# Hybrid decoder block: rotary tables made early, with the sine's table set loaded near the beginning, the rows filled in v's ring and the transposes in the middle of the first accumulation

## The chip, the cores and the metric

The kernel runs on one core of a Trainium2 chip. The metric is the device time of one execution in microseconds (us). A profiled execution also gives a span, which begins with the first and ends with the last instruction of the core.

## The reference, cut to what matters

One layer of a decoder block, for one sequence of 1024 tokens of width 1024. The conditioning vector gives six modulation vectors; the first two scale and shift the normalised input.

```
cond = silu(c);  mod = cond @ w_ada + b_ada          # six parts
h    = rms_norm(x, g_attn_pre) * (1 + sc_a) + sh_a
proj = h @ w_in                                      # q, k, v of mixers A and B
ang  = positions * inv_freq                          # 8 frequencies
q, k = partial_rope(q, k, cos(ang), sin(ang))        # first 16 of 64 dims
oa   = sliding-window attention with sinks           # 8 query, 2 key heads
ob   = mixture of three dilated windows              # 8 heads
x    = x + gt_a * rms_norm(concat(norm(oa), norm(ob)) @ w_out)
x    = x + gt_m * rms_norm(relu(h2 @ w_up)**2 @ w_down)
```

All of it is float32 in and out. The kernel multiplies each operand as a high and a low half, three matmuls to a product.

## The kernel before, in words

**A planner writes the order.** `Sched` (L175) holds a queue for each of ScalarE (ACT), VectorE (DVE), GpSimd (POOL) and the DMA queue (SP), and several streams for TensorE (PE). Each step, made by `op` (L196) or `pe_op` (L208), has a duration that the author wrote down, the events that it depends on, the ring buffers that it takes and gives back (`Res`, L161), and a priority. `run` (L272) advances model clocks and emits whichever step can start first; the priority only breaks ties. So the written durations decide the order in which instructions stand on each engine, and an edit early in the program can reorder what follows. Once emitted, an engine works strictly in that order, and waits at its head for semaphores.

**The opening stage.** SP loads `x` in eight blocks of 128 tokens, the first 2048 columns of `w_ada` in sixteen pieces and the first unit's weights (`order0`, L471). `x_block` (L610) squares a block on ACT (L613), makes 1/rms on POOL (`rsqrt_mean`, L452: L457 and L459), scales the block on ACT or DVE (L617, L618), transposes it on PE (L625) and copies it to `xnT` (L629). `mod_group(g)` (L634), g from 0 to 3, sums `w_ada` times `cond` on DVE (L645, L647), adds over partitions on PE (L655), makes scale and shift on DVE (L661 to L663), and calls `mod_chunk` (L672) for the chunks k = 2g and 2g+1 of the model width: high half on ACT (L684), full value on ACT (L681), low half on DVE (L687). `split_w` (L536) splits the weights, with the high half on ACT (L539) and the low half on DVE or POOL (L544).

**The first unit's accumulation.** `first_unit` (L883) keeps six accumulators in PSUM: x = 0, 1 (token halves) by c = 0, 1, 2 (128 columns each). Chunks k = 0 to 5 are added as they come; the chunks 6 and 7 follow tile by tile, starting with x = 0, c = 0 (the tail). Each chunk and tile is two matmuls with the high half of h (L861, L862) and one with the low half (L864). PE fills idle time before that with matmuls on ones (`filler`, L871, L878). One of the two buffers of the PSUM pool `pt` belongs to an accumulator from the second half of chunk 0 on.

**The rotary tables.** DVE reduces the angles (`f_turns`, L590). `f_sin` (L604) makes sine (L605) and cosine (L606) and then runs an Exp (L607), so that the table set of Exp is back in place. It waits for the angles and for all of `e_xn`, with priority 8. DVE negates the sine (L697). `tables` (L700) then, for the cosine and the sine: POOL sets a tile `rows` (L707) and copies the 8 columns to their places, ten copies each (L713); PE transposes it in two groups of four, one for each x (L719); ACT scales each group into `tab` (L721). The tile comes from the ring "wa" of `p0` (six buffers). A second call (L949), for mixer B, comes with unit 2.

**Behind a tile.** `evac` (L734): for c = 0 DVE rotates the PSUM tile with the tables (L757 to L760, the rope), ACT makes the high half (L763), DVE or POOL the low half (L766). For c = 1, 2 ACT and DVE make the halves (L774, L777). The halves `hl` lie in the ring "stg" of five tiles, which the loads of the second part of `w_ada` (`wa_st`, L994) use as well. SP then copies them row by row into `kt` and `qt` (L803): twelve DMAs for each x of the first unit. The v part goes through ACT (`vt`, L825), PE (L831) and ACT and DVE (L839, L842) into the ring "v" of three buffers. `proj_tile` (L915) makes the tiles of the units 1 to 5 in the two buffers of the pool `pj`, L861 to L864 again.

**Attention** opens (`open_attention`, L955) when the tables and all chunks are planned; it loads the masks (L971). The first scores (L1177) need all twelve DMAs of unit 0, x = 0. After them the matmuls of the projections and those of attention alternate, and the output projection and the MLP follow. The MLP is made of seven half-size products (P1 to P7) in place of eight for each block (L1897 to L1899).

## Time and profile before

| what | us |
|---|---|
| median of three runs (1161.61 to 1167.61) | 1163.08 |
| the profiled execution's own time | 1161.99 |
| its span | 1160.2 |
| PE busy | 1117.1 |
| first unit's projection, last matmul issued | 66.94 |
| unit 1's first two tiles, last matmul issued | 77.10 |
| first scores | 83.00 |

The opening stage is the first 67 us. The matmuls of the other projections (L861 into `pj`) stand from 67.2 to 391.4 us, beside attention; those of the output projection (L1473) from 413 to 530; the MLP's begin at 530. A row of the timeline gives start, length, engine, line, operation, output and inputs, count, and in brackets the idle time of the engine before it and what ended that. A matmul's length overlaps with the next: distances between starts are what they cost.

### The profile page before, as it was taken

To read this page: it belongs to the slowest core of one execution; us is meant where nothing else is said; L and a number is where in the kernel's file an instruction comes from. 1 tells how busy PE (TensorE), PEld (TensorE's weight loads), DVE (VectorE), ACT (ScalarE), POOL (GpSimd) and SP (SyncE) were. 2 spreads that over 40 slices of the span, in tenths; PEclk is the share of its full clock that TensorE was granted. 3 is DMA by queue.
4 is the path that set the end of the run, shared out by engine and by line. 5 is a ranking of instruction groups with operands and counts; after the bars stand their busy time and mean duration, and the time that the engine had idled before them with its cause. 6 is when DMAs were issued, how large, how long until landed. Compare 5 with 4: busy or idle time off the path is not lost.

```text
span 1160.2 us, 15646 instructions
## 1 busy us (share of the span) xinstructions
PE 1117.1 (96%) x5416; PEld 926.6 (80%) x5416; DVE 815.4 (70%) x1380; ACT 639.2 (55%) x1105; POOL 261.1 (23%) x344
## 2 busy tenths in 40 slices
PE   8989989999999899998999999999999999999996
PEld 7768778788888787887788888888888888888885
DVE  7848576566666775658969665499653796547998
ACT  7949676455555774667676524563233732246542
POOL 2347667566663441112000000000000000000002
PEclk9989989999999989999999999999999999999998
DMA  9477857465545614554683057812369212585103
GB/s 351 161 174 168 168 120 182 111 153 122 134 102 130 156 48 139 193 181 182 257 314 118 19 207 274 315 50 89 120 220 326 106 55 73 184 306 181 37 19 146
DMA packets 90944, 185.31 MB, mean 160 GB/s; under 512 B 8432, under 2 KB 31088, under 8 KB 90864
## 3 DMA queue, kind: packets, MB, share of 16 engines
q1 hardware_dynamic: 90864, 184.30, 51.1%
q8 instruction: 43, 0.70, 0.3%
q14 instruction: 37, 0.30, 0.1%
HBM read 137.08 MB, written 28.31 MB: 143 GB/s over the span
## 4 chain that ended last, share of the span: by engine, by line
PE 70%; DVE 10%; DMA 7%; issue 4%; POOL 4%; ACT 3%; SPq 2%; DVEq 0%; POOLq 0%; ACTq 0%
PE mlp_ps L1898 16%; PE mlp_ps L1899 16%; PE mlp_ps L1897 16%; PE pj L861 3%; PE pj L864 3%; PE pj L862 3%; PE s_ps L1122 2%; PE o_ps L1257 1%; DMA wa<-in_w_ada 1%; SPq L803 1%; PE pt_ps L1227 1%; DMA wa_st<-in_w_ada 1%; DVE hw L1668 1%; PE pt_ps L1230 1%; PE s_ps L1177 1%
## 5 line engine op out<-in xcount | busy, mean ns | idle before, releaser
L1897 PE MATMUL mlp_ps<-hw 128*128 128x512 f32 x896 | 349.7, 390 | 1.2 <-ACT hw L1659 1.2
L1898 PE MATMUL mlp_ps<-hw 128*128 128x512 f32 x896 | 348.7, 389 | 1.1 <-DVE hw L1665 1.1
L1899 PE MATMUL mlp_ps<-hw 128*128 128x512 f32 x896 | 348.6, 389 | 0.0
L1897 PEld LDWEIGHTS mlp_ps<-hw 128*128 128x128 f32 x896 | 168.2, 188 | 36.8 <-ACT hw L1659 1.6
L1898 PEld LDWEIGHTS mlp_ps<-hw 128*128 128x128 f32 x896 | 168.2, 188 | 36.8 <-DVE hw L1665 1.4
L1899 PEld LDWEIGHTS mlp_ps<-hw 128*128 128x128 f32 x896 | 168.2, 188 | 34.9
L1668 DVE TENSOR_TENSOR hw<-w,hw 128x1024 fp32r<-128x1024 f32 x96 | 114.5, 1219 | 94.7 <-ACT hw L1661 94.4
L1661 ACT CAST hw<-w 128x1024 fp32r<-128x1024 f32 x96 | 97.5, 1047 | 129.8 <-PE mlp_ps L1899 97.5
L1997 POOL TENSOR_TENSOR st<-st,nhalf 128x1 f32<-128x1 f32 x8 | 7.8, 978 | 601.9 <-DVE st L1995 601.9
L861 PE MATMUL pj<-hw,w_hl 128*128 128x512 f32 x240 | 104.2, 434 | 0.0
L864 PE MATMUL pj<-hw,w_hl 128*128 128x512 f32 x240 | 95.5, 398 | 0.0
L862 PE MATMUL pj<-hw,w_hl 128*128 128x512 f32 x240 | 95.3, 397 | 0.0
L1245 DVE TENSOR_TENSOR ph<-pt_ps,ph 128x512 fp32r<-128x512 f32 (+1 forms) x110 | 69.7, 648 | 36.0 <-ACT ph L1241 35.7
L1661 ACT CAST hw<-u 128x1024 fp32r<-128x1024 f32 x48 | 48.7, 1052 | 64.6 <-PE mlp_ps L1899 64.6
L1241 ACT CAST ph<-pt_ps 128x512 fp32r<-128x512 f32 (+1 forms) x110 | 59.5, 555 | 32.1 <-PE pt_ps L1230 27.0
L1668 DVE TENSOR_TENSOR hw<-u,hw 128x1024 fp32r<-128x1024 f32 x48 | 57.0, 1218 | 18.2 <-ACT hw L1661 18.2
L1148 ACT ACTIVATE p_sb<-p_sb,mn 128x128 f32<-128x128 f32 (+3 forms) x64 | 49.7, 777 | 36.3 <-DVE mn L1141 34.9
L1955 DVE TENSOR_TENSOR yacc<-yacc,mlp_ps 128x512 f32<-128x512 f32 x96 | 62.1, 681 | 3.3 <-PE mlp_ps L1899 3.3
L1153 POOL TENSOR_SCALAR p_sb<-p_sb,den 128x128 f32<-128x128 f32 (+3 forms) x64 | 49.0, 775 | 47.8 <-DVE den L1151 44.6
L1010 POOL TENSOR_TENSOR ada_acc<-ada_acc,wa_st 128x512 f32<-128x512 f32 x42 | 55.5, 1320 | 3.5
L864 PEld LDWEIGHTS pj<-hw,w_hl 128*128 128x128 f32 x240 | 45.6, 190 | 10.7
L1473 PE MATMUL y_ps<-hw,oh 128*128 128x512 f32 x128 | 51.7, 404 | 0.0
(205 smaller groups left out, 2010.6 us busy)
## 6 DMA issues: line engine op xcount, KB each, us to landing
hw<-s_dram SPq DMA_DIRECT2D x84, 512.0 KB
wa_st<-in_w_ada SPq DMA_DIRECT2D x32, 512.0 KB
w<-in_w_up SPq DMA_DIRECT2D x32, 512.0 KB
w<-in_w_down SPq DMA_DIRECT2D x32, 512.0 KB
s_dram<-hw SPq DMA_DIRECT2D x28, 512.0 KB
w_st<-in_w_in SPq DMA_DIRECT2D x36, 256.0 KB
x_sb<-in_x SPq DMA_DIRECT2D x16, 512.0 KB
wa<-in_w_ada SPq DMA_DIRECT2D x32, 256.0 KB
```

What stands on the lines that cost most here:

```text
L861: T.matmul(ps, w[:, 0, n], h[0], start=(k == 0), stop=False)
L862: T.matmul(ps, w[:, 1, n], h[0], start=False, stop=False)
L864: T.matmul(ps, w[:, 0, n], h[1], start=False, stop=(k == KC - 1))
L1010: G.tensor_tensor(ada.acc[:, :512], ada.acc[:, :512], wa[:, j], ALU.add)
L1241: A.copy(b["ph"][:, 0, :w], b["pt"][:, :w])
L1245: V.tensor_tensor(b["ph"][:, 1, :w], b["pt"][:, :w], b["ph"][:, 0, :w].bitcast(F32), ALU.subtract)
L1661: A.copy(out[j][0], flat(src[j]))
L1668: V.tensor_tensor(out[j][1], flat(src[j]), out[j][0].bitcast(F32), ALU.subtract)
L1897: T.matmul(ps[m][:], sh, mh, start=starts and k == 0, stop=False, **kw)
L1898: T.matmul(ps[m][:], sh, ml_, start=False, stop=False, **kw)
L1899: T.matmul(ps[m][:], sl, mh, start=False, stop=k == 3, **kw)
L1955: e = op("DVE", t_dv(512), lambda: V.tensor_tensor(y(), y(), ps[m][:], ALU.add), [e, ml.e_y[tb, n]], gives=gives, prio=1)
```

## The change

The changed kernel adds two steps and moves three.

- A new step loads the table set of the sine: one activation with Sin on a small constant tile, behind the first Exp (the silu) and the initialisation, priority 0.
- `f_sin` no longer waits for `e_xn`. It waits for the angles and the step above, with priority 1, and its trailing Exp is gone. The negation follows it, also with priority 1.
- A new step with priority 8 runs an Exp on the small tile, behind the sine and the low halves of chunk 7. It brings the table set of Exp back.
- The first call of `tables` takes its `rows` from the ring "v" instead of "wa". Filling them waits for the sine and for all eight 1/rms steps of `x_block`. The transposes also wait for the high half of chunk 3 (`e_hh[3, 1]`). Both calls' transposes get that event; for the second call it is long past.

```diff
+    warm = p0.tile([P, KC], F32, name="warm")
+    e_sinset = op("ACT", 1.5, lambda: A.activation(warm[:], nhalf[:], AF.Sin), [e, e_init], prio=0)
...
     def f_sin():
         A.activation(sinw[:, :, 1], ang[:], AF.Sin)
         A.activation(cosw[:], kq[:], AF.Sin)
-        A.activation(ang[:], kq[:], AF.Exp)
-    e_ang, e_xn = e, [[], []]
+    e_xn, e_rs = [[], []], []
+    e_sin = op("ACT", 0.5, f_sin, [e, e_sinset], prio=1)
+    e_rope = op("DVE", 0.15, lambda: V.tensor_scalar(sinw[:, :, 0], sinw[:, :, 1], -1.0, None, ALU.mult), [e_sin],
+                prio=1)
...
         e = rsqrt_mean(rstd[:, tb:tb + 1], ssq[:, tb:tb + 1], e)
+        e_rs.append(e)
...
-    e = op("ACT", 3.2, f_sin, [e_ang] + e_xn[0] + e_xn[1], prio=8)
-    e_rope = op("DVE", 0.15, lambda: V.tensor_scalar(sinw[:, :, 0], sinw[:, :, 1], -1.0, None, ALU.mult), [e],
-                prio=8)
...
-                t = b["t"] = place()[:].rearrange("p (b r) -> p b r", b=TB)
+                t = b["t"] = place(i)
...
-            e = op("POOL", 4.0, f_rows, [e_rope], takes=[(r_place, 1)], prio=0)
+            e = op("POOL", 4.0, f_rows, [e_rope] + e_rs, takes=[(r_place, 1)] if r_place else [], prio=0)
...
-                d = pe_op("tab", 0.43, f_t, [e], takes=[(r_bank, 1)], gives=[(r_place, 1)] if x else [])
+                d = pe_op("tab", 0.43, f_t, [e, e_hh[3, 1]], takes=[(r_bank, 1)], gives=[(r_place, 1)] if x and r_place else [])
...
-    tables([(0, 2, 4), (1, 2, 1)], lambda: place0("rows"), r_wa, r_t,
+    tables([(0, 2, 4), (1, 2, 1)], lambda i: vring.tile([P, TB, P], F32, name="rows", tag="v"), r_v, r_t,
            lambda: pt.tile([P, 4, P], F32, name="ptab", tag="t"), [[], []])
+
+    op("ACT", 1.6, lambda: A.activation(warm[:], nhalf[:], AF.Exp), [e_sin] + [e_hl[KC - 1, x] for x in range(2)],
+       prio=8)
```

More of the change, by code (lines that the diff above doesn't have):

```diff
@@ L948, in feed_proj @@
                     e_.clear()
-                tables([(0, 1, 4)], lambda: stage("rows"), r_stg, r_x,
+                tables([(0, 1, 4)], lambda i: stage("rows")[:].rearrange("p (b r) -> p b r", b=TB), r_stg, r_x,
                        lambda: px.tile([P, 4, P], F32, name="ptab", tag="x"), [[e_rot[1, 0]], [e_rot[1, 1]]])
```

## The prediction

> **What bounds the kernel now.** I read the page's first lines, then the windows of the first 200 us, because the change touches the opening stage and what follows from it.
>
> ```profile
> span 1160.2 us, 15646 instructions
> ...
> PE 1117.1 (96%) x5416; PEld 926.6 (80%) x5416; DVE 815.4 (70%) x1380; ACT 639.2 (55%) x1105; POOL 261.1 (23%) x344
> ```
> ```profile
> 36.00:57.00 21.00, 21.00 (x100) 17.62 (x101) 17.74 (x29) 18.84 (x22) 9.82 (x21) 1.00 0.42 136
> 57.00:67.00 10.00, 10.00 (x54) 8.25 (x52) 6.13 (x10) 5.87 (x11) 3.44 (x3) 1.00 0.44 152
> 67.00:77.30 10.30, 10.30 (x48) 8.07 (x46) 3.56 (x6) 3.33 (x8) 7.31 (x10) 1.00 0.82 183
> 77.30:83.00 5.70, 0.18 (x1) 0.03 (x1) 1.55 (x3) 0.52 (x1) 0.00 (x0) 0.82 0.85 182
> 83.00:90.00 7.00, 7.00 (x30) 5.72 (x31) 4.27 (x17) 4.24 (x15) 2.84 (x6) 0.66 0.80 157
> 90.00:120.00 30.00, 29.49 (x176) 25.13 (x175) 26.19 (x83) 27.39 (x81) 24.58 (x41) 1.00 0.77 177
> 120.00:200.00 80.00, 74.34 (x398) 61.50 (x396) 51.64 (x146) 55.06 (x145) 53.18 (x85) 0.96 0.68 154
> ...
> 143.50:148.70 5.20, 0.18 (x1) 0.00 (x0) 3.79 (x10) 4.58 (x10) 3.42 (x4) 0.72 0.31 100
> 148.70:153.00 4.30, 4.29 (x19) 3.89 (x20) 1.99 (x9) 1.97 (x8) 4.17 (x9) 0.54 0.41 100
> ```
>
> Columns: stretch, length, busy PE, weight load, DVE, ACT, POOL, then PE's granted clock. PE is busy without a break from 36 to 77, stands still for 5.5 us, works 7 us at a mean clock of 0.66, and is full again until 143.5, where a second stop comes. So the time is PE's work plus its stops, and a stop costs twice: 7.00 x (1 - 0.66) = 2.4 us after the first, 4.30 x (1 - 0.54) = 2.0 us after the second. A change in the opening stage is worth what it takes from or adds to PE's waits. Past about 200 us the orders of both kernels agree on every engine but for a few swaps, so the rest (MLP included) only shifts.
>
> The timeline shows what the first stop waits for, in PE, DVE and SP rows.
>
> ```profile
> 57.09 0.60 PE L719 MATMUL ptab<-head,rows 128*128 128x128 f32 x4
> 57.44 0.48 PE L861 MATMUL acc<-hw,w_hl 128*128 128x512 f32 x1
> ...
> 59.04 0.48 PE L864 MATMUL acc<-hw,w_hl 128*128 128x512 f32 x1
> ...
> 83.00 1.94 PE L1177 MATMUL s_ps<-kt,qt 128*128 128x128 f32 x8 [5.51 <-DMA kt<-hl]
> ...
> 148.71 0.69 PE L831 MATMUL pv<-head,vt 64*128 64x64 f32 x4 [5.02 <-ACT tab L721]
> ```
> ```profile
> 62.57 0.68 DVE L757 TENSOR_TENSOR hl<-acc,tab 64x512 f32<-64x512 f32 x1 [3.70 <-ACT tab L721]
> ```
> ```profile
> 64.81 0.44 SPq L994 DMA_DIRECT2D wa_st<-in_w_ada  x1
> ...
> 67.47 1.78 SPq L803 DMA_DIRECT2D kt<-hl  x2
> 69.31 8.35 SPq L803 DMA_DIRECT2D qt<-hl  x10
> 77.75 1.32 SPq L803 DMA_DIRECT2D kt<-hl  x2
> 79.16 7.46 SPq L803 DMA_DIRECT2D qt<-hl  x10
> ```
> The chain of waits has the last of the twelve by itself:
>
> ```profile
> 77.06 0.59 SPq L803
> ```
>
> The tile of x = 0, c = 0 is complete at about 59.4 (the L864 at 59.04 ends it), but its rope starts at 62.57, when the sine's table arrives from ACT. SP then issues the twelve DMAs of x = 0 from 67.47 to 77.66, and the scores start at 83.00. The tables are late by 3.1 us, and the scores hang on them.
>
> **The change, part by part.**
>
> *The sine on ACT.* Rows of ACT, POOL and DVE:
>
> ```profile
> 5.60 1.06 ACT L613 ACTIVATE junk<-x_sb 128x1024 bf16<-128x1024 f32 x1 [1.05 <-DMA x_sb<-in_x]
> ...
> 32.60 1.55 ACT L684 ACTIVATE hw<-xnT,s_a,g_a 128x512 fp32r<-128x512 f32 x2
> ...
> 37.71 2.37 ACT L681 ACTIVATE xnT<-xnT,s_a,g_a 128x1024 f32<-128x1024 f32 x2
> ...
> 41.13 1.28 ACT L605 ACT_TABLE_LOAD   x1
> 42.42 0.26 ACT L605 ACTIVATE sinw<-ang 128x64 f32<-128x64 f32 x1
> ...
> 42.84 1.28 ACT L607 ACT_TABLE_LOAD   x1
> 44.14 0.26 ACT L607 ACTIVATE ang<-kq 128x64 f32<-128x64 f32 x1
> 44.88 2.38 ACT L684 ACTIVATE hw<-xnT,s_a,g_a 128x1024 fp32r<-128x1024 f32 x2 [0.48 <-DVE s_a L663]
> ```
> ```profile
> 28.10 0.57 POOL L459 TENSOR_TENSOR rstd<-rs_t,nhalf 128x1 f32<-128x1 f32 x1
> ...
> 42.96 4.77 POOL L713 COPY rows<-cosw 128x64 f32<-128x64 f32 x10 [9.00 <-ACT cosw L606]
> 47.67 0.95 POOL L707 MEMSET rows<- 128x1024 f32 x1
> 48.69 3.02 POOL L713 COPY rows<-sinw 128x64 f32<-128x64 f32 x4
> 52.49 1.14 POOL L713 COPY rows<-sinw 128x64 f32<-128x64 f32 x6 [0.78 <-DVE sinw L697]
> ...
> 63.12 1.29 POOL L544 TENSOR_TENSOR w_hl<-w_st,w_hl 128x512 fp32r<-128x512 f32 x1 [0.16 <-ACT w_hl L539]
> ```
> ```profile
> 46.89 1.52 DVE L647 SCALAR_TENSOR_TENSOR acc_a<-wa,cond,acc_a 128x512 f32<-128x512 f32 x2
> ```
>
> Two table loads and the small activations behind them leave ACT at 41.13 to 44.40. ACT then stood idle for 0.48 us until DVE's shift came, so their going is worth nothing by itself. Early, one load and a tiny activation fall before 5.60, where ACT idled 1.05 us: the first square moves by about 0.35 us. The two sines (0.5 us) come behind the angles. I walked ACT, DVE, POOL and PE through the new order with these durations: ACT's lead on the first chunks is up to 1.4 us later, the planner gives DVE one scaling more, and by the second half of chunk 0 ACT is even again (32.2 against 32.6) while DVE is 0.8 us late, which puts PE about 0.7 us behind. The last `w_ada` loads slip by 0.7 us too; DVE uses the last of them at 46.89, well after they land, so that is covered. The third load (1.28 us) now stands on ACT ahead of two splits and the rope's cast, behind the last chunk, where ACT waits anyway: nothing.
>
> The Trainium skill, "ScalarE: Activation LUTs", section "What ACT_TABLE_LOAD costs", counts a drain of about 1.38 us on top of each load. The row at 42.42 starts 0.01 us behind the load, and no drain is seen; with it the first square would be 1.4 us later still, and the sum worse by at most that.
>
> *The rows on POOL* now start behind the eighth 1/rms, at about 28.9. A copy took 0.48 us (4.77 / 10) beside a busy DVE, 0.755 (3.02 / 4) beside DVE's low halves, 0.19 (1.14 / 6) with DVE idle. With 0.48 the cosine is ready at 28.9 + 0.95 + 4.8 = 34.7 and the sine, at something between 0.48 and 0.755, at 40.5 to 43.2. PE asks for them at 38.0 and 42.2: a wait of 0 to 1.0, taken as 0. At 0.755 throughout, the sine is ready at 28.9 + 1.9 + 15.1 = 45.9.
>
> *The transposes on PE.* Four groups of 0.35 us (57.44 - 57.09) leave the tail and go to chunks 1 and 2: 1.4 us earlier work, none saved. In the middle they share one PSUM buffer, so each waits for ACT's copy of the one before. ACT's copy stands behind L681 of the chunks 2 and 3 (ended 40.08), and PE comes to the second group at 40.5: just even. Adding 0.7 and 1.4 us, with small waits, the tail starts at 59.1 instead of 57.09.
>
> *The rope.* The tile is complete six matmuls into the tail. A matmul costs 0.23 us (10.30 us for the 48 from 67.00 to 77.30, four of them short): 59.1 + 6 x 0.23 = 60.5, and the tables are there since about 45. The rope starts at 60.6 instead of 62.57. POOL has a weight half (1.29 us) ahead of the rope's low half, which costs 0.2. SP's first `kt` issue: 65.7 instead of 67.47.
>
> *SP and the DMAs.* In the new order the masks go out before 60 and `wa_st` behind all 24 DMAs of unit 0; the last weight tile still goes ahead. Of the 24, the first twelve took 10.2 us (67.47 to 77.66) with those loads under way, the second twelve 8.9 (77.75 to 86.62). I take 8.9, so the twelfth is issued 8.2 us after the first; from there to the scores it was 83.00 - 77.06 = 5.9. Scores: 65.7 + 8.2 + 5.9 = 79.8; without the gain, 65.7 + 15.5 = 81.2.
>
> *PE's wait.* The new order puts 30 matmuls of unit 1 ahead of the scores, not 48, and both small v transposes. So 18 x 0.23 = 4.1 us of work is left over, and 0.4 is done. The balance is (79.8 - 83.0) + 4.1 - 0.4 = **+0.5 us**, or +1.9 without SP's gain. But the stop is now in two parts. The v transposes of x = 1 wait for a `hl` tile, and so for the first six DMAs: about 3.8 us. Then come six matmuls, then about 0.9 us. In the trace the clock fell some 3.6 us after PE stopped:
>
> ```profile
> 80.00:82.00 2.00, 0.00 (x0) 0.00 (x0) 0.60 (x1) 0.00 (x0) 0.00 (x0) 0.73 0.97 203
> ...
> 88.00:90.00 2.00, 2.00 (x14) 1.82 (x13) 1.20 (x5) 1.48 (x5) 0.84 (x3) 1.00 1.02 164
> ```
>
> (0.73 is 0.54 of the stretch at half clock, so from 80.9.) I take it that the clock mostly holds, which saves the 2.4 us. Sum: 0.5 - 2.4 = **-1.9 us**. The Trainium skill, "TensorE: Matmul & The Clock Gate", section "What's actually happening", says that the gate closes after an idle window of about 3.4 us that runs free of the kernel. By that rule 3.8 us of idle covers a whole window only rarely; the trace agrees with its 3.6 us.
>
> *Second stop.* PE waits at 148.7 for ACT's first table of mixer B, which stands behind a `hl` tile waiting for DMAs. The new order has 1.4 us less PE work ahead of it, but ACT has two activations (1.3 us) less as well. I take no change.
>
> **Rivals.**
>
> *The clock falls again (A).* If PE's wait stays in one piece, or the 3.8 us cover the gate, the sum is +0.5 to +1.9. For it: both stops before, 5.0 and 5.5 us, did close it. Time 1163.6 to 1165.0.
>
> *The rows are late (B), slower.* PE stands in order at the sine's first group while POOL copies. Place: 42.2. It decides from 30.85 + 20 c > 42.2, so from 0.57 us a copy, between the two rates seen. At 0.755 PE waits 3.7 us, ACT's tables and behind them the chunks 4 and 5 slip as much, and the gain of the tail is gone: -1.9 + 3.7 = +1.8, or +4.2 with the clock closed once more, 1167.3. If the second stop lengthens too, by the 1.4 us that PE has less ahead of it, and the `hl` tiles, all five now held by unit 0, hold unit 1 as long as they do before (5.0 us at 148.7 a second time), it passes 1169.
>
> *The second stop goes as well (D), faster.* Attention starts 3 us earlier against ACT, DVE and POOL, each busy for 24 to 27 of the 30 us after 90, and unit 1's DMAs go out some 4 us earlier. If that covers the 5.0 us and 2.0 of slow clock at 143.5, the time is -1.9 - 7.0 = -8.9. Against it: that wait follows unit 1's own last tile, which PE makes.
>
> *Nothing happens* is within A: the scores hang on SP and not on the tables.
>
> **How the numbers follow.** The profiled execution took 1161.99, 1.1 us less than the median of 1163.08; -1.9 makes 1160.1 of it, and of the median **1161.2**. About 0.5% (5.8 us) is what a measurement of this kernel can tell from no change. Chances: forecast 0.42 (1158 to 1163), A 0.20, B 0.18, D 0.20 (1154.2). D and the forecast's lower end lie below 1157.3: faster 0.24. The worse part of B and unforeseen waits of the reordered attention lie above 1168.9: slower 0.15. Same 0.61. The range leaves out the far half of D and of B: 1154.5 to 1167.5.
>
> **What would show it.** Right: transposes of the tables between 38 and 45, rope at 60 to 61, first `kt` issue near 65.7, scores near 80, clock 1.00 from 83 to 90. Wrong: a PE wait of over 1 us released by POOL's rows or ACT's table near 42 (B); a stop of 5 us in one piece before the scores (A); no stop between 140 and 150 (D), or a longer one.

## The result and the profile after

The changed kernel took **1170.35 us** (median of 13 runs, 1167.6 to 1176.46) against 1163.08 for the kernel before on the same chip (13 runs): a ratio of 1.0059, interval 1.004 to 1.0078. It is slower by about 0.6%, where the forecast was 1161.2 and no difference that can be measured. The profiled execution took 1169.35 with a span of 1167.6, so it is 7.4 us longer in span than the one of before (1161.99, span 1160.2).

The first lines of the page after:

```profile
span 1167.6 us, 15645 instructions
...
PE 1120.3 (96%) x5417; PEld 927.9 (79%) x5417; DVE 818.1 (70%) x1380; ACT 637.4 (55%) x1105; POOL 263.1 (23%) x345
```

PE's idle time (span less busy) went from 1160.2 - 1117.1 = 43.1 to 1167.6 - 1120.3 = 47.3. The other 3.2 us are busy time. By the clock records PE worked 21.6 us at half clock against 18.0 before, which makes 1.8 of them; the other 1.4 were not followed. The windows of the same stretches as before show where (columns as in the prediction; the last two are the DMA engines' busy share and GB/s):

```profile
36.00:57.00 21.00, 20.63 (x107) 17.28 (x108) 17.70 (x28) 16.67 (x20) 4.02 (x5) 1.00 0.53 170
57.00:67.00 10.00, 10.00 (x46) 8.25 (x44) 6.76 (x10) 6.57 (x11) 6.34 (x5) 1.00 0.30 102
67.00:77.30 10.30, 6.63 (x31) 4.94 (x29) 3.13 (x6) 2.71 (x5) 3.49 (x6) 1.00 0.76 126
77.30:83.00 5.70, 3.69 (x12) 2.57 (x13) 1.70 (x3) 0.96 (x2) 0.00 (x0) 0.70 0.86 150
83.00:90.00 7.00, 7.00 (x45) 6.04 (x45) 6.20 (x27) 5.18 (x21) 3.33 (x8) 1.00 0.80 143
90.00:120.00 30.00, 27.33 (x152) 23.33 (x151) 21.44 (x69) 25.60 (x76) 21.70 (x33) 0.94 0.67 156
120.00:200.00 80.00, 73.51 (x400) 60.12 (x399) 53.12 (x147) 53.19 (x141) 54.83 (x90) 1.00 0.65 156
200.00:300.00 100.00, 94.45 (x520) 79.34 (x518) 59.38 (x155) 49.55 (x106) 60.47 (x66) 0.97 0.57 131
```

Up to 90 us the new kernel is no worse: the stretch 83 to 90, at a mean clock of 0.66 before, now runs at 1.00. The loss comes behind that: PE is busy 27.33 us of the 30 after 90 (29.49 before, and at 1.00 instead of 0.94), and 94.45 of the 100 after 200, where the window of before reads:

```profile
200.00:300.00 100.00, 96.86 (x548) 81.88 (x547) 61.57 (x161) 49.77 (x105) 59.23 (x63) 0.98 0.59 134
```

PE's timeline gives the stops (L1177, L831 and L864 of before are L1182, L836 and L869 here). All PE rows after 60 and before 300 us with a wait of 0.6 us or more, behind three of the opening stage:

```profile
36.37 0.96 PE L869 MATMUL acc<-hw,w_hl 128*128 128x512 f32 x3 [1.57 <-DVE hw L692]
37.63 0.60 PE L721 MATMUL ptab<-head,rows 128*128 128x128 f32 x4
...
43.75 0.63 PE L721 MATMUL ptab<-head,rows 128*128 128x128 f32 x4
...
78.49 0.69 PE L836 MATMUL pv<-head,vt 64*128 64x64 f32 x4 [4.85 <-ACT vt L830]
...
82.78 1.08 PE L1182 MATMUL s_ps<-kt,qt 128*128 128x128 f32 x8 [0.83 <-DMA qt<-hl]
...
95.30 1.10 PE L1182 MATMUL s_ps<-kt,qt 128*128 128x256 f32 x4 [2.48 <-DMA qt<-hl]
...
127.69 0.63 PE L1182 MATMUL s_ps<-kt,qt 128*128 128x128 f32 x4 [2.27 <-DMA o_dram<-ot]
...
150.73 0.46 PE L836 MATMUL pv<-head,vt 64*128 64x64 f32 x4 [2.26 <-ACT tab L723]
...
164.40 0.74 PE L1182 MATMUL s_ps<-kt,qt 128*128 128x256 f32 x4 [1.73 <-DVE mn L1197]
...
208.46 0.58 PE L1262 MATMUL o_ps<-ph,v_hl 128*128 128x256 f32 x1 [3.21 <-ACT ph L1246]
209.75 0.58 PE L1262 MATMUL o_ps<-ph,v_hl 128*128 128x256 f32 x1 [0.71 <-DVE ph L1250]
...
265.47 0.33 PE L1232 MATMUL pt_ps<-head,p_sb 128*128 128x128 f32 x1 [1.12 <-POOL p_sb L1158]
```

Nine waits from 60 to 300, 19.5 us in sum. Before had four there: the two that the prediction shows (5.51 and 5.02), 0.64 at 171.98 and 2.52 at 207.70, 13.7 in sum. The large second stop has shrunk from 5.02 to 2.26. Those at 95, 128, 164 and 265 are new, and at 208 to 210 two waits of 3.92 together stand where before has this one:

```profile
207.70 1.12 PE L831 MATMUL pv<-head,vt 128*128 128x128 f32 x4 [2.52 <-DVE ot L1293]
```

The last matmul of the projections (L864 before, L869 after, into `pj`) tells that next to nothing is lost later. First before, then after:

```profile
391.95 0.40 PE L864 MATMUL pj<-hw,w_hl 128*128 128x512 f32 x1
```
```profile
399.18 0.40 PE L869 MATMUL pj<-hw,w_hl 128*128 128x512 f32 x1
```

That is 7.23 of the 7.4 us. I added up from PE's records what is lost from the start to a given time: its idle time, and half of the time that it worked at clock 0.50. In us, each row from the one profiled execution, with five kernels of the experiments below:

```
lost up to      90    100    140    160    200    300    400    600
before        12.0   12.0   12.5   19.5   20.1   24.8   26.8   41.9
after         11.6   15.8   18.2   20.5   22.4   30.8   31.3   47.9
e9            12.6   12.6   13.2   19.6   20.6   26.0   27.3   45.5
e10           14.2   18.1   23.2   26.4   26.8   36.5   37.1   54.0
e12           14.9   15.0   17.2   18.1   19.2   23.7   25.2   45.9
e17           11.9   11.9   12.2   12.9   14.0   17.0   20.4   34.3
e18           11.3   11.3   11.6   12.5   14.7   16.9   21.1   35.8
```

After is 0.4 us ahead at 90, 3.8 behind at 100, 5.7 behind at 140, only 1.0 behind at 160 (before's second stop lies there), and 6.0 behind at 300 and at 600.

**Two of the new stops, followed back.** *At 95.30* PE comes to the first scores that need q of x = 1. In before the same group starts at 95.02 and waits for nothing:

```profile
95.02 0.73 PE L1177 MATMUL s_ps<-kt,qt 128*128 128x256 f32 x4
```

The ten q transfers of x = 1 had left SP by 86.62 in before and by 87.04 in after, so they come no earlier. But after has less work ahead of that group: PE had worked 95.02 - 12.0 = 83.0 us there in before and 95.30 - 14.1 = 81.2 in after, idle time and half of the slow time taken off. So it waits, and then works 3.4 us at half clock.

*At 208.46* PE waits for ACT's `ph`. The rows of ACT, POOL and SP, in that order:

```profile
206.68 0.62 ACT L539 CAST w_hl<-w_st 128x512 fp32r<-128x512 f32 x1 [5.20 <-DMA w_st<-in_w_in]
207.32 0.58 ACT L1309 COPY otmp<-o_ps 64x512 f32<-64x512 f32 x1
207.93 0.48 ACT L1246 CAST ph<-pt_ps 128x384 fp32r<-128x384 f32 x1
```
```profile
199.42 1.29 POOL L544 TENSOR_TENSOR w_hl<-w_st,w_hl 128x512 fp32r<-128x512 f32 x1
```
```profile
65.96 1.39 SPq L808 DMA_DIRECT2D kt<-hl  x2
...
200.74 0.33 SPq L530 DMA_DIRECT2D w_st<-in_w_in  x1
```

ACT stands 5.20 us at the split of a weight tile whose load SP issued only at 200.74, 0.03 us after POOL had ended the low half of an earlier tile (199.42 + 1.29 = 200.71) and given its buffer back; `ph` and so PE wait behind that split. In before two weight loads went out together at 192.28; ACT's split of the first waited 1.68 us, that of the second not at all. The order on ACT is the same there. What differs is the engine of that earlier low half. In before DVE made it, 0.3 us behind ACT's high half (which ended at 190.64):

```profile
190.96 0.78 DVE L544 TENSOR_TENSOR w_hl<-w_st,w_hl 128x512 fp32r<-128x512 f32 x1
```

In after the planner gave it to POOL, where other steps stand ahead, and it starts 5.4 us behind ACT's half (193.98 to 199.42). Four of the kernels shown here have that lag (after, e4, e5 and e10, 5.4 to 5.7 us), and in these ACT waits 5.2 to 6.2 us for the load behind it; in all others the lag is at most 0.5 us and the wait at most 1.6.

### The profile page after: what moved, and what is told of

It is laid out like the page before. It is cut to its first block, busy times and chain, and to the rows that moved or that the text cites. A ratio compares the mean times of both kernels' runs of the same rounds, so it can differ in the third digit from the quotient of the medians.

```text
span 1167.6 us, 15645 instructions
## 1 busy us (share of the span) xinstructions
PE 1120.3 (96%) x5417; PEld 927.9 (79%) x5417; DVE 818.1 (70%) x1380; ACT 637.4 (55%) x1105; POOL 263.1 (23%) x345
## 4 chain that ended last, share of the span: by engine, by line
PE 70%; DVE 10%; DMA 6%; POOL 5%; issue 4%; ACT 3%; SPq 1%; DVEq 0%; POOLq 0%; ACTq 0%
PE mlp_ps L1903 16%; PE mlp_ps L1902 16%; PE mlp_ps L1904 16%; DMA qt<-hl 3%; PE pj L866 3%; PE pj L869 2%; PE pj L867 2%; PE s_ps L1127 2%; PE o_ps L1262 1%; PE y_ps L1478 1%; PE pt_ps L1232 1%; PE y_ps L1480 1%; PE y_ps L1479 1%; POOL ada_acc L1015 1%; DVE hw L1673 1%
## 5 line engine op out<-in xcount | busy, mean ns | idle before, releaser
L869 PE MATMUL pj<-hw,w_hl 128*128 128x512 f32 x240 | 95.6, 398 | 0.0
L869 PEld LDWEIGHTS pj<-hw,w_hl 128*128 128x128 f32 x240 | 45.6, 190 | 10.7
```

The source lines that it names most:

```text
L869: T.matmul(ps, w[:, 0, n], h[1], start=False, stop=(k == KC - 1))
```

## The experiments

The question was first which of three causes it is: **(a)** something in front of the scores (the transposes in the middle, the transfers of `kt` and `qt`, the work that PE has left while it waits for them); **(b)** one part of the early tables by itself (the sine, or the rows in v's ring); **(c)** the order that the planner dealt anew to everything behind. Each expectation names the theories as they stood when it was written.

### Parts of the change, and the planner's picture of the transfers (e1 to e4)

e1: the transposes wait for the last low half, so that they fall behind the tail's start again.

```diff
-                d = pe_op("tab", 0.43, f_t, [e, e_hh[3, 1]], takes=[(r_bank, 1)], ...
+                d = pe_op("tab", 0.43, f_t, [e, e_hl[KC - 1, 1]], takes=[(r_bank, 1)], ...
```

> The changed kernel, with the sine and the rows early, but the table transposes held until the last modulated chunk, as late as in the kernel before. Theory 1 (the early tables make the planner place PE's attention work ahead of the DMAs that feed it): 45 matmuls of unit 1 instead of 30 stand ahead of the first scores, the stop at 95 us goes, and the time is near that of the kernel before, 1161 to 1166 us. Theory 2 (the early work on ACT and POOL costs): stays at 1168 to 1171. Theory 3 (any change of the planner's input deals the attention's order anew, with stops that come out as they come): anywhere from 1160 to 1172.

Measured 1175.66 (before on that chip 1165.63), ratio 1.0084, interval 1.0059 to 1.011. Slower still, against the 1161 to 1166 expected by the theory that the loss lies in front of the scores, and above what any of the three theories allowed (1172). It is no clean undoing: the scores start at 88.59 there, later than in either kernel, and the stops behind them lie at other places again (3.95 us at 118, 4.35 at 158.7).

e2 (on after) and e3 (on before): only the planner is told that each transfer of `kt` and `qt` lands 4 us later than it thinks. No step is added or taken away.

```diff
-            end = self.dma + 0.8
+            end = self.dma + (0.8 if o.prio != -12 else 4.8)
```

> The changed kernel, with one figure of the planner: kt and qt transfers are taken to land 4.8 us behind their time on the queue instead of 0.8 (in the trace the last of x = 0 lands 6.5 us behind its issue). 48 matmuls of unit 1 then stand ahead of the first scores instead of 30. Theory 1: the stops at 78 and 95 us (4.9 + 0.8 + 2.5 us, and 1.4 + 1.7 us of half clock behind them) shrink to one of about 1 to 3 us, and the time falls by 3 to 6 us, 1164 to 1167. Theory 2: no change, 1169 to 1171. Theory 3: anywhere from 1160 to 1172.

> The kernel before with the same figure of the planner. 48 matmuls of unit 1 and one more group of v transposes stand ahead of the first scores instead of 42. Theory 1: its first stop (5.5 us and 2.4 us of half clock) shrinks by 1.4 to 2 us, the rest stays: 1159 to 1163. Theory 2: 1161 to 1163. Theory 3: anywhere from 1158 to 1172.

e2: 1166.22, ratio 1.0006 (0.999 to 1.0022). e3: 1161.55, ratio 0.9965 (0.9947 to 0.9983). The same figure takes 0.35 to 0.55% off either kernel, and with it the new kernel is level with before. In e3 PE still stops three times for over 1 us up to 300 us:

```profile
84.30 1.94 PE L1177 MATMUL s_ps<-kt,qt 128*128 128x128 f32 x8 [3.31 <-DMA qt<-hl]
...
131.30 2.05 PE L1269 MATMUL o_ps<-ph,v_hl 128*128 128x512 f32 x4 [3.57 <-DVE den L1201]
...
206.86 0.66 PE L831 MATMUL pv<-head,vt 128*128 128x128 f32 x4 [2.55 <-DVE ot L1293]
```

The second stop isn't at 148 but at 131, on another line: a figure in the planner moves stops about.

e4: rows from the old ring "wa", and so only behind the scaling of all of x; the early sine stays.

```diff
-            e = op("POOL", 4.0, f_rows, [e_rope] + e_rs, takes=...
+            e = op("POOL", 4.0, f_rows, [e_rope] + e_xn[0] + e_xn[1], takes=...
-                d = pe_op("tab", 0.43, f_t, [e, e_hh[3, 1]], takes=...
+                d = pe_op("tab", 0.43, f_t, [e], takes=...
-    tables([(0, 2, 4), (1, 2, 1)], lambda i: vring.tile([P, TB, P], F32, name="rows", tag="v"), r_v, r_t,
+    tables([(0, 2, 4), (1, 2, 1)], lambda i: place0("rows")[:].rearrange("p (b r) -> p b r", b=TB), r_wa, r_t,
```

> The changed kernel, with the rows in the ring of the w_ada tiles and behind all evictions of x, instead of in v's ring; the transposes still come in chunks 1 and 2 and 30 matmuls still stand ahead of the first scores. Theory 1: as the changed kernel, 1168 to 1172. Theory 2: 1168 to 1171, less whatever v's ring costs. Theory 3: anywhere from 1160 to 1172.

1169.33, ratio 1.0032 (1.0013 to 1.0051). Without v's ring it is slower than before as well, so v's ring isn't the whole cause. Whether half of the loss has gone with it can't be read from one dealt order against another.

### The twelve transfers, and an unrelated figure (e5 to e8)

e5 (on after) and e6 (on before): of unit 0, the transfers of q's high halves are issued from ACT's queue, the others from SP.

```diff
-                                nc.sync.dma_start(o, src if both else src[:, s_])
+                                (nc.scalar if u == 0 and s_ == 0 else nc.sync).dma_start(o, src if both else src[:, s_])
```

> The changed kernel in the same order on PE, DVE and POOL, with the high halves of unit 0's q (five of the twelve DMAs of each x) issued by ACT, which makes them, instead of SP. It asks whether SP's row of DMAs sets the time of the first scores. Theory 1 (the scores hang on SP and the DMAs, so that early tables reach nothing): SP needs 7 x 0.85 = 6 us instead of 10.3 for the twelve, and the scores come at 77 to 80 instead of 82.8; the stops at 78 and 95 us shrink by 4 to 6 us together and the time falls to 1163 to 1167. Theory 2 (the early work on ACT and POOL costs) and theory 3 (the attention's order on PE, dealt anew, holds the stops): the first stop goes but the later ones stay, at least 1167.

> The kernel before with the same five DMAs of each x on ACT's queue, other orders unchanged. Theory 1: the scores come 3 to 4 us earlier, at 79 to 80, and the first stop of 5.5 us shrinks to about 2; the clock may hold: 1157 to 1161. The difference between this and the changed kernel with two queues then tells what the tables are worth when SP is no longer the bound: theory 1 says that the changed kernel is level or faster. Theory 3: a difference of any sign, 3 to 7 us, as between the two kernels as they are.

e5: 1172.8 (before 1165.79), ratio 1.0057 (1.0038 to 1.0076). e6: 1165.27, ratio 0.9977 (0.9959 to 0.9995). (The ratios are those on record and not quotients of the medians, which would give 0.9996 for e6, and 1.0037 for e8 below.) In e5 the scores were expected between 77 and 80; PE's timeline has them where they were ("issue" means that the profile shows no releaser):

```profile
82.81 1.94 PE L1182 MATMUL s_ps<-kt,qt 128*128 128x128 f32 x8 [2.77 <-issue]
```

The twelve took from 67.05 to 76.5 with two issuing engines, 9.4 us, against 10.3 (65.96 to 76.24) from SP alone; from first issue to scores it was 15.8 and 16.8. In e6 they came at 81.92, 13.9 us behind the first issue (68.00) against 15.5 in before, where 79 to 80 was expected. So a second issuing engine takes 1.0 to 1.6 us off that way, and the rest of it is not the issuing. The Trainium skill, "DMA: Bandwidth & Descriptors", section "Issuing engines are not separate DMA queues", says that transfers started by different engines run on the same 16 DMA engines and that only the issuing time is saved; the trace of e5 agrees (0.9 us less to issue the twelve, 1.0 less to the scores).

e7 (on after) and e8 (on before): the planner's price of a projection step, 2% up. No step is touched.

```diff
-            d = dense(0.681, emit, [w_e[u, w_at(u, c, k)[0]]], ...
+            d = dense(0.697, emit, [w_e[u, w_at(u, c, k)[0]]], ...
```

> The changed kernel with one figure of the planner that has nothing to do with the tables: three matmuls of unit 1 and later are priced 0.697 us instead of 0.681 (the trace has 0.23 each). Theory 3 (each new input deals the attention's order anew): the time moves by 2 us or more either way, 1162 to 1176. Theories 1 and 2: within 2 us of the changed kernel, 1168 to 1172.

> The kernel before with the same price of 0.697 us. Theory 3: the time moves by 2 us or more either way, 1155 to 1170. Theories 1 and 2: within 2 us of the kernel before, 1161 to 1165.

e7: 1168.95, ratio 1.0021 (1.0 to 1.0042). e8: 1170.09, ratio 1.0025 (1.0007 to 1.0043). The same figure makes the old kernel slower and the new one less slow. On the old kernel alone two figures of the planner gave 0.9965 and 1.0025: the two orders lie 0.6% apart, as much as the change that is to be explained. That brought cause (c) to the front, but says nothing yet of what the tables do by themselves.

### The order held fixed (e9 to e12)

Here the planner's choice is taken out. The order of the steps is written into the file, and the run loop takes the next one of that list:

```diff
+            best = self.planned()
             if best is None:
                 return
```

This lets the two halves of the change be set apart. e9 has after's opening, with early sine, early rows and transposes in the middle, up to the first matmul of unit 0's tail, and from there before's order on every engine. e10 has before's code and opening, and from the tail on after's order. (Line numbers in such kernels are 49 higher than in the kernel they stem from.)

> The changed kernel up to the tail of unit 0 (early sine, rows in v's ring, transposes in chunks 1 and 2), and from the tail on every engine's order written out as in the kernel before, so that the planner can't deal it anew; the load for Exp stands at the head of the tail. Theory 3, now as: what the change costs is the order dealt after the tail, the tables cost nothing themselves: no slower than the kernel before, 1160 to 1166 us where that takes 1163 to 1166; the rope starts near 61 and the stops are those of before or shorter. Theory 2 (the early tables and their work cost by themselves): near the changed kernel, 1169 to 1173.

> The other corner: the kernel before up to the tail (late sine, rows and transposes), and from there on every engine's order as in the changed kernel. Theory 3: it has the changed kernel's stops at 78, 95, 127, 164 and 208 us, or longer ones, and takes 1169 to 1175 us. Theory 2: near the kernel before, 1161 to 1166. Both in part: 1166 to 1169.

| tables | order behind the tail | us (before on that chip) | ratio and interval |
|---|---|---|---|
| late | old (before) | 1163.08 | 1 |
| early | old (e9) | 1165.77 (1166.29) | 1.0000, 0.9979 to 1.0022 |
| late | new (e10) | 1173.49 (1166.29) | 1.0070, 1.0045 to 1.0094 |
| early | new (after) | 1170.35 (1163.08) | 1.0059, 1.004 to 1.0078 |

**The whole loss goes with the order; within 0.2% the early tables cost nothing and bring nothing.** In PE's rows e9 has the stops of before and e10 those of after. First e9:

```profile
83.33 1.94 PE L1231 MATMUL s_ps<-kt,qt 128*128 128x128 f32 x8 [5.00 <-DMA qt<-hl]
...
147.92 0.69 PE L885 MATMUL pv<-head,vt 64*128 64x64 f32 x4 [3.27 <-ACT tab L772]
```

and e10:

```profile
98.26 1.19 PE L1226 MATMUL s_ps<-kt,qt 128*128 128x256 f32 x4 [3.04 <-DMA wa_st<-in_w_ada]
...
213.28 0.38 PE L1306 MATMUL o_ps<-ph,v_hl 128*128 128x256 f32 x1 [4.16 <-ACT ph L1290]
```

The stop at 213.28 is after's stop at 208.46: in ACT's rows of e10 the split of the weight tile ahead of `ph` waits 6.15 us for a load that SP issued at 204.88. In e9, with before's order, two loads went out at 192.71 and no such stop is seen. In e9 the rope starts at 61.44, 1.1 us earlier than in before, and SP's first `kt` at 66.52, 0.95 earlier; the scores are at 83.33, 0.3 later. The lead of the tables is gone in the transfers.

e11: after's opening, then the order of e3.

> The changed kernel up to the tail, and from there on the order of the kernel before with the landing figure of 4.8 us (the run that took 1161.55 where before took 1165.63). Theory 3: the early tables bring what is left of their 1 to 2 us where the order is good: 1158 to 1162, below both kernels. Theory 2: 5 us above that run, 1165 to 1168.

1161.61, ratio 0.9968 (0.9948 to 0.9989), against 0.9965 for e3 with late tables. A second pair with the same answer: early or late makes no difference. e3 and e11 are quicker than both kernels, without any change of what is computed or sent.

e12: after's order up to the first matmul of unit 2 (142 us), then before's. If the new stops were independent of each other, only those up to 142 should remain.

> The changed kernel in its own order up to the first matmul of unit 2 (142 us in its trace), and from there on every engine's order as in the kernel before. It asks where in the order the loss lies. By the work that PE has done by then, the changed kernel is 5.9 us behind at 140 (the stops at 95 and 128 us) and gains 4.1 back at 143 to 151, where the kernel before has its stop of 5.0 us; from 160 to 220 it loses 4.1 more (stops at 164 and 208 us). If the stops are local and add up, the late part is the old one again and the time falls to 1165 to 1168. If what is handed on at 142 us sets the rest (loads and the ada pieces behind), it stays at 1169 to 1173.

1173.65 (5 runs, 1169.04 to 1175.02; before 1165.08), ratio 1.0076 (1.0059 to 1.0094): nothing was won back. Its profiled run, the quickest of the five, shows two things. Up to 142 it has after's order, but no stop at 95: there the stop before the scores was followed by 10.2 us at half clock, and the loss up to 100 is 15.0 where after's was 15.8. With a fast clock after waits at 95, with a slow one it doesn't, and loses as much. Behind 142, in before's order, the stops at 164 and 208.46 to 209.75 are gone, one of 3.06 stands at 209.34 on the row on which before waits 2.52 at 207.70, and up to 300 it has lost 23.7, less than before (24.8). Most of the loss then comes at the first matmul of the output projection, where before has no such wait, with slow clock around it (10.2 us from 409 to 423, in before 6.8):

```profile
418.22 0.80 PE L1527 MATMUL y_ps<-hw,oh 128*128 128x512 f32 x1 [4.10 <-ACT oh L1485]
```

ACT's `oh` waits for a load that SP issued at 411.87, behind the gate's load, whose ring buffer POOL had held until 411.4. In before these two loads went out at 403.28 and 406.12. So the stops don't add up one by one: what an order saves in one place another wait takes back, and a mixed order has waits of its own. Which part of after's order makes the loss can't be had by cutting it in two.

### What sets the scores (e13 to e18)

If earlier tables bring nothing because the transfers eat the lead, fewer or better transfers should bring something, and then early tables perhaps too. e13 and e14 send seven transfers in place of twelve for x = 0 of unit 0 (of q only the high half; the rest of the tile is cleared by DVE, so a correction of the scores is left out), in e9's order (e13) and in before's (e14). e15 and e16 are the same with the clearing on POOL.

```diff
-                                nc.sync.dma_start(o, src if both else src[:, s_])
+                                if u or x or s_ != 1:
+                                    nc.sync.dma_start(o, src if both else src[:, s_])
...
+        qs[0, 0] = qring.tile([P, 4, 512], F32R, name="qt", tag="qt")
+        V.memset(qs[0, 0][64:128].bitcast(F32), 0.0)
```

> Early tables with the old order (e9), and five of the twelve transfers of unit 0, x = 0 left out: those of the low halves of q, so that a correction of the scores is missing; DVE clears that part of the tile once, all else in the same order. If the transfers of x = 0 set the time of the scores, they start 3 to 5 us earlier than in e9, at 78.5 to 80.5, the first stop shrinks from 5.0 to 0.5 to 2 us, its slow clock goes, and the time falls by 4 to 6 us, to 1160 to 1162 where before takes 1166. If something else holds the scores (the ring of five tiles, SP's waits), they stay within 1 us of 83.

> The kernel before in its own order, with the same five transfers left out and the same clearing. If the transfers hide the early tables in e9, the tables now show: the scores start 1 to 2 us later than in e13, at 80 to 82, and the time is 1 to 3 us above it. If the early tables are worth nothing even then, both start within 0.5 us and take the same time.

> As e13 (early tables, old order, the low halves of q of unit 0, x = 0 not sent), with the clearing on POOL instead of DVE. The rope starts at 61.5 as in e9 and kt is issued near 66.6. If the transfers are all that hides the tables, the scores start near 79 and the time is 1 to 3 us below e16. If the tables are worth nothing even so, it is level with e16.

> As e14 (late tables, the kernel before's order, the same transfers left out), with the clearing on POOL. kt near 67.4, scores at 80 to 80.5, time as e14: 1158 to 1161 where before takes 1164.

| run | tables | us (before) | ratio and interval | first `kt` issue to scores, us |
|---|---|---|---|---|
| e13 | early | 1161.64 (1163.62) | 0.9984, 0.9968 to 1.0 | 68.23 to 80.52: 12.3 |
| e14 | late | 1159.54 (1163.62) | 0.9965, 0.9947 to 0.9982 | 67.32 to 80.36: 13.0 |
| e15 | early | 1164.8 (1165.72) | 0.9987, 0.9975 to 0.9999 | 70.24 to 81.99: 11.8 |
| e16 | late | 1160.38 (1165.72) | 0.9953, 0.9937 to 0.997 | 68.01 to 80.00: 12.0 |

The last column was 15.5 in before and 16.8 in after and e9: the scores follow the transfers, and five transfers are worth 2.5 to 5 us there (in e14 PE itself was the last to come, without a wait). But of the early tables these runs say nothing. The clearing was put at the head of the attention, and with early tables it stood in front of what mattered: in e13 it took DVE 1.76 us at 61.70, just ahead of the rope, and in e15 it stood on POOL ahead of the weight halves. The first `kt` issue was later with early tables than with late ones both times, so these pairs compare the clearing's place and not the tables.

e17 and e18 change the pieces instead. In before and after q goes out in pieces of 8, 8, 24, 8 and 16 rows, each as a high and a low half, and k in one piece to two places, which makes twelve transfers for each x; here q goes in 16, 32 and 16 rows, the same bytes in eight transfers. k stays as it was, so q's features stand in another order than k's: both kernels leave out the matching order, and their scores are not those of the reference. e17 has before's order, e18 that of e9.

```diff
-PARTS_A = (((0, 32, 2, "q", 0), (64, 32, 2, "q", 32), (1, 64, 2, "k", 0)),
-           ((0, 96, 1, "q", 8), (96, 32, 1, "q", 40)), ((0, 64, 1, "q", 48),))
+PARTS_A = (((0, 64, 2, "q", 0), (1, 64, 2, "k", 0)),
+           ((0, 128, 1, "q", 16),), ((0, 64, 1, "q", 48),))
```

> The kernel before in its own order, with q of units 0 and 1 sent in pieces of 16, 32 and 16 rows instead of 8, 8, 24, 8 and 16 (per half). The same bytes go out; q's features then stand in another order than k's, so the scores are not those of the reference. The Trainium skill, DMA: Bandwidth & Descriptors, section Why a DMA increments its semaphore by 16 and not by 1, says that a transfer is spread over the largest number of the 16 engines that divides its rows: 8 for 8 and 24 rows. If that uneven load is what holds the transfers, kt to scores falls from 15.5 to 11 to 13 us, the scores start near 80 and the time falls by 2 to 6 us below before. If the bytes alone hold them (2 KB packets inside the SBUF), kt to scores stays above 14.5 and the time is within 2 us of before.

> The same pieces of q with the early tables and the old order (e9). kt is issued near 66.5, 0.9 us ahead of e17. If the transfers were all that hid the early tables, the scores start 0.5 to 1.5 us ahead of e17 or PE arrives later than they do, and the time is 0.5 to 2 us below e17. If the early tables are worth nothing anyway (PE's own 48 matmuls then end last), both take the same time within 1 us; if they cost something of their own, e18 is above e17.

e17: 1155.6 (before 1166.6), ratio **0.9910**, 0.9885 to 0.9935. e18: 1155.86, ratio **0.9917**, 0.99 to 0.9934. These are the largest effects of the study. The windows of 73 to 77.3 us, the middle of the transfers of x = 0, first of before, then of e17 (third and second column from the right: granted clock, DMA share):

```profile
73.00:77.30 4.30, 4.30 (x20) 3.38 (x18) 0.69 (x1) 0.68 (x2) 1.67 (x4) 1.00 0.62 122
```
```profile
73.00:77.30 4.30, 4.30 (x21) 3.54 (x20) 0.69 (x1) 0.60 (x1) 2.92 (x6) 1.00 1.08 164
```

The DMA share is 1.08 instead of 0.62 (it sums the packets' times, so it can pass 1). The Trainium skill, "DMA: Bandwidth & Descriptors", section "Why a DMA increments its semaphore by 16 and not by 1", says that a transfer is spread over as many engines as the largest number up to 16 that divides the rows on both sides. By that rule the pieces of 8 rows go to 8 engines, that of 24 to 12 (not 8, as the expectation has it), and those of 16 and 32 to 16. The trace agrees: in before a transfer of 8-row pieces raised its semaphore 9 times (once 1.0 to 2.1 us behind the issue, 8 times from 3.5 us on), one of 24 rows 13 times, one of 16 rows 16 times, and in e17 each one 16 times. PE's stops in e17 between 60 and 210:

```profile
82.58 1.94 PE L1226 MATMUL s_ps<-kt,qt 128*128 128x128 f32 x8 [4.57 <-DMA kt<-hl]
...
197.23 0.39 PE L1306 MATMUL o_ps<-ph,v_hl 128*128 128x256 f32 x1 [0.90 <-DVE ph L1294]
...
201.99 0.66 PE L880 MATMUL pv<-head,vt 128*128 128x128 f32 x4 [1.63 <-DVE ot L1342]
```

The scores came only 0.4 us earlier than in before (they were expected near 80), and the first stop is there still: 14.7 us from first issue to scores (67.86 to 82.58), which the expectation gave to transfers held by their bytes alone. The last transfer of x = 0 landed at 82.50 in before and at 82.45 in e17. But the second stop and the slow clock behind it are gone, as the table of lost time shows (12.9 against 19.5 at 160), and 6.6 of the 7.6 us that e17 has gained by 600 lie there. That this comes from unit 1's transfers, the others with new pieces, is argued and not shown; nor do these runs part the even rows from the smaller number of transfers, eight in place of twelve. e18 against e17 is the third pair on the early tables, and the one with the cleanest opening:

```profile
81.42 1.94 PE L1231 MATMUL s_ps<-kt,qt 128*128 128x128 f32 x8 [3.48 <-DMA kt<-hl]
```

Here the tables' lead does reach the scores, 1.16 us (81.42 against 82.58), and it is kept to the end of the output projection (last matmul at 523.07 against 524.41). The medians are the same nevertheless: in the profiled run one more stretch at half clock, 3.4 us from 554.9 on, costs 1.7 at the opening of the MLP. About 1 us, or 0.1%, is what early tables can be worth, and these runs can't tell that from nothing.

## Why the prediction was wrong

By its steps:

1. *The sine on ACT*: right. The first square starts at 5.27 (0.33 earlier, 0.35 predicted), and the load is followed by its activation 0.01 us later; no drain is seen here either:

```profile
3.51 1.28 ACT L579 ACT_TABLE_LOAD   x1
4.80 0.21 ACT L579 ACTIVATE warm<-nhalf 128x8 f32<-128x8 f32 x1
5.27 1.06 ACT L617 ACTIVATE junk<-x_sb 128x1024 bf16<-128x1024 f32 x1 [0.26 <-DMA x_sb<-in_x]
```

   PE waits 1.57 us at 36.37 for the second half of chunk 0, 0.74 more than before (0.7 predicted).

2. *The rows on POOL*: right that they are in time, and rival B is refuted. In POOL's rows a copy took 0.30 and 0.43 us, below the 0.48 that was taken, and no PE row waits for them:

```profile
29.65 3.04 POOL L715 COPY rows<-cosw 128x64 f32<-128x64 f32 x10
...
33.65 4.25 POOL L715 COPY rows<-sinw 128x64 f32<-128x64 f32 x10
```

3. *The transposes and the rope*: right. The four groups lie between 37.63 and 43.75, the tail starts at 59.26 (59.1 predicted), the rope at 60.82 (60.6), SP's first `kt` at 65.96 (65.7):

```profile
60.82 0.68 DVE L762 TENSOR_TENSOR hl<-acc,tab 64x512 f32<-64x512 f32 x1 [1.93 <-PE acc L869]
```

4. *SP and the DMAs*: wrong, and with it the scores by 3.0 us. The twelfth was issued 9.7 us after the first, not 8.2 (65.96 to 75.65), and from there to the scores it was 7.1, not 5.9 (to 82.78); 0.3 came from the later start. Fewer loads beside them did not make them faster. So the scores moved by 0.2 us only, from 83.00 to 82.78, not to 79.8.

5. *PE's wait*: it did come in two parts (4.85 and 0.83), and the clock was full from 83 to 90, as predicted; but the 4.85 alone closed the gate, from 78.3 to 81.7, so "the clock mostly holds" was wrong and part of the work between was slow (0.70 in 77.3 to 83). The count of leftover matmuls was wrong too: the 48 rows of before between 67 and 77.3 are 42 matmuls of unit 1, four v transposes and the end of unit 0. (Six matmuls of unit 1's first two tiles come behind the first scores, so these tiles don't end at 77.10.) So 42 - 30 = 12 were left over, 2.8 us instead of 4.1. Together with step 4 the balance at 90 us is 0.4 us to the good where 1.9 was predicted. This error is small.

6. *The second stop*: it shrank from 5.02 to 2.26 us at full clock; from 140 to 160 us after loses 2.3 us where before loses 7.0, which is two thirds of rival D; "no change" was wrong, on the good side.

**The step that failed** is the one that ended the sum at the scores and the second stop: "Past about 200 us the orders of both kernels agree on every engine but for a few swaps, so the rest (MLP included) only shifts." Behind about 390 us it does only shift, and next to nothing is lost there. But the same order is not the same waiting: the stop at 208.46 lies in a stretch whose order on ACT is unchanged, and goes back to one low half that had moved from DVE to POOL just ahead of it (199.42) and to the weight load behind that. And between 90 and 200 us, where the planner had dealt anew, the sum had a price for one stop alone. By the table after loses 6.1 us against before from 90 to 140, wins 4.7 back up to 160 and loses 5.0 from there to 300; the sum had none of the three. The new order there was known and left to "unforeseen waits of the reordered attention", within a chance of 0.15. The 2 x 2 of e9 and e10 shows that this was the whole result. Rival B's 1167.3 and more was close in time, but with a mechanism that the trace refutes.

**Shown**: that the loss belongs to the order behind the tail (e9, e10, e11), that the early tables by themselves change nothing measurable, that the scores wait for transfers (e13 to e16) and only for 1.0 to 1.6 us for the issuing engine (e5, e6). **Only argued**: the way from POOL's low half to the stop at 208.46, which rests on the rows of after, e4, e5 and e10 against those of the other kernels, without an edit of its own; and that the even rows made the gain of e17, and not the smaller number of transfers. **Open**: which items of the order make the stops at 127.69 and 164.40, and which part of after's order is to blame, since cutting it in two brought a new stop (e12).

## What to carry to other kernels

Where a planner deals the order from written durations, an edit is two changes: what it does, and a new draw for everything behind. Figures that had nothing to do with the tables moved the old kernel by -0.35% and +0.25%, so one draw proves little about an edit of that size; hold the order fixed by writing it out, exchange one half at a time, and only then price the edit. And before making something earlier, ask what is late next: here the twelve transfers were, then the next twelve, and to send them in eight pieces whose rows 16 divides, in place of twelve, moved the time by 0.9%, which no earlier table did (in kernels that leave out k's matching order of rows; with it, nothing was tried).

## What the runs showed of the hardware that was not expected

The clock fell after shorter stops than the prediction took (3.6 us). Three windows of after: the 3.3 us ahead of the stop at 95.30, the 3.4 us behind it, and the 3.4 us behind the stop of 2.27 us at 127.69:

```profile
92.00:95.30 3.30, 0.82 (x5) 0.36 (x3) 0.89 (x7) 0.26 (x3) 0.00 (x0) 1.00 1.00 246
95.40:98.80 3.40, 3.40 (x17) 3.40 (x18) 2.09 (x6) 2.83 (x7) 2.50 (x3) 0.50 1.06 260
...
127.70:131.10 3.40, 3.40 (x15) 2.57 (x16) 1.07 (x5) 1.40 (x5) 1.29 (x2) 1.00 1.02 310
```

A stop of 2.48 us cost 3.4 us at half clock, one of 2.27 us nothing; in e14 a stop of 1.51 us was followed by 3.4 us at 0.50. In the traces of all 20 kernels the slow stretches between 60 and 600 us are 3.4, 6.8 or 10.2 us long, multiples of 3.4. The Trainium skill, "TensorE: Matmul & The Clock Gate", section "What's actually happening", counts an idle window of about 3.4 us; the length of the slow stretches agrees. That a window with 0.82 us of work in 3.3 still closed the gate shows that it needn't be idle throughout, and so a stop can't be priced by its length alone. In each trace the slow stretches begin whole multiples of 3.41 us apart (78.32, 95.39 and 208.03 in after). Cut along that grid, the 20 traces hold 3024 windows at full clock between 60 and 600 us. All 66 with less than 1.49 us of PE work were followed by half clock, 25 of the 76 from there to 2.12 us, and none with more. So it matters how a stop falls across the grid: that of 2.27 us at 127.69 fell into two windows, with 2.73 and 1.83 us of work. A stop of 3.8 us, as the prediction had it, leaves at most 3.41 - 1.9 = 1.5 us of work in one of two windows, so it would mostly have closed the gate.
